# The end of a macaron encoder layer: the last product's sums, row scalings and stores in an order of their own

## The chip, the cores and the metric

The kernel runs on one core of one Trainium2 chip. The metric is the device time of one execution in microseconds (us). The profile is one execution, recorded by the hardware profiler; its span is the time from the first to the last instruction. TensorE does the matmuls, VectorE (DVE), ScalarE (ACT) and GpSimd (POOL) the elementwise work, and SyncE (SP) issues transfers.

## The reference, cut to what matters

Two sequences of 512 tokens with 1024 channels go through one encoder layer in float32, each by itself:

```python
x = x + 0.5 * swiglu(rms_norm(x, ffn1_norm), ffn1_w_gate, ffn1_w_up, ffn1_w_down)
...  # attention and mLSTM branches, merged, added to x
x = x + 0.5 * swiglu(rms_norm(x, ffn2_norm), ffn2_w_gate, ffn2_w_up, ffn2_w_down)
return rms_norm(x, final_norm)
```

where `rms_norm(x, g)` is `x * rsqrt(mean(x*x) + 1e-6) * g` over the 1024 channels, and `swiglu(x)` is `(silu(x @ w_gate) * (x @ w_up)) @ w_down` with 2816 hidden channels. The change is in the last line of this, the final norm, and in how the reciprocal root of every norm is worked out.

## The kernel before, in words

Every float32 matmul is done as three passes of rounded parts (high x high, high x low, low x high). Both sequences go through a feed-forward together, and the two-by-two product of (sequence, half) blocks is done with seven block products in place of eight, named B11, B21, T2, T3, T4, T1 and B22. The sums of these products give the four blocks of the result.

`ffn_down` (L435) is the second matmul of a feed-forward. It goes over four chunks of hidden channels, and in each over the seven products in the order of `DOWN` (L430): 28 steps. A step has four groups d = 0 to 3, one for each block of 128 tokens; a group ends in one PSUM bank, and `flush_` (L527) takes it from there: DVE adds half of it to an accumulator in SBUF (L536). In the last chunk the accumulators become the finished rows: `xs[s][:, h*4 + b]` holds sequence s, half h of the channels, block b of the tokens, 128 x 512 numbers. The finished blocks come in this order, and for each `done(s, h, b)` is called: B21 gives (0, 0), T4 gives (0, 1), T1 gives (1, 1), and B22, the very last step, gives (1, 0). So the first sequence is complete after T4, and the second block by block during B22. `e16` and `e5` are accumulators that are no longer needed in the last chunk, once their values have been added.

`done2` (L1328) ends the second feed-forward. For each block ACT squares it and sums the squares along the row into `ssq3[s]` (L1145, `square`); then POOL multiplies it by the gain `fn[h]` in place (L1331), or DVE where (s, h) is (1, 0). The multiply writes where the square reads, so it comes behind the square. When a row's two halves are there, `row_scale` (L1150) adds the two sums of squares and `rstd_cols` (L149) makes the reciprocal root r on DVE: mean plus epsilon, a first guess from the bits (a shift, a subtraction from a constant), and three rounds of three Newton instructions each, 12 small instructions, 13 with the sum. For the first sequence this is done once, for four blocks, behind its last square; for the second in two pairs of blocks, behind d = 1 and d = 3 of B22. Each block of 128 rows is then scaled by r, 128 x 1024 in one instruction, on ACT (L1345), the last block on DVE (L1343), and stored with one 512 KB transfer that SP issues (L1346). `rstd_cols` is called by all other norms of the kernel too: 21 calls in all, among them the first normalisation of each sequence (`norm_x`, L1173) and the eight memory heads, whose r TensorE broadcasts (`bcast_psum`, L181).

What sets the order: the program's instructions are put into one queue per engine by a scheduler at build time. It goes by priority, which is program order unless `shifted` changes it, and by when it believes the operands ready; an instruction that is ready goes ahead of an earlier one that isn't. On the chip each engine runs its queue strictly in order. `pin` (`tc.keep_in_program_order`, L1118) keeps the instructions that it is given in program order among each other on their engine. Nothing in `done2` is pinned before the change. The small tiles of `rstd_cols` take turns in five buffers (tag `rs4`).

Of the kernel before, what the change touches and what calls it, by code (L numbers as in the profile page):

```python
# [26 lines left out]
def encoder(ctx, tc, I, outs):  # L27
# [14 lines left out]
    def nm(s):  # L42
        n_id[0] += 1
        return f"{s}_{n_id[0]}"
# [98 lines left out]
    def emit_hl(src, g, k, xh, xl):  # L143
# [2 lines left out]
                                       op0=ALU.mult, op1=ALU.subtract)  # L146
        return i1, i2

    def rstd_cols(v, width, n):  # L149


        def t_(dt=F32):
            w = max(width, 4)
            return spool.tile([P, w], dt, tag=f"rs{w}", bufs=5, name=nm("rs"))[:, 0:width]
        V = nc.vector
        a = t_()
        V.tensor_scalar(a, v, 1.0 / n, EPS, op0=ALU.mult, op1=ALU.add)
        b = t_(I32)
        V.tensor_scalar(b, a.bitcast(I32), 1, None, op0=ALU.logical_shift_right)
        y_ = t_(I32)  # L160
        V.tensor_scalar(y_, b, -1.0, 1597463007.0, op0=ALU.mult, op1=ALU.add)
        y = y_.bitcast(F32)
        for _ in range(3):
            t = t_()
            V.scalar_tensor_tensor(t, y, -0.5, y, op0=ALU.mult, op1=ALU.mult)
            V.tensor_tensor(t, t, a, op=ALU.mult)
            r = t_()
            V.scalar_tensor_tensor(r, t, 1.5, y, op0=ALU.add, op1=ALU.mult)
            y = r
        return y  # L170

    def col_sums(acc, bs=(0, 1, 2, 3)):
        p = PT()
# [258 lines left out]
    DH = KD // 2  # L432
    n_steps = len(DOWN) * len(CHUNKS)

    def ffn_down(wd, rb, ring, tail, xres, done, at_step, hook):  # L435
# [91 lines left out]
        def flush_(i, d, p):  # L527
# [2 lines left out]
                   T3: xs[1][:, DH + d], B22: xs[1][:, d]}[m]  # L530
            if last and m == T1:
                acc = xs[1][:, DH + d]
            if i < 7 and m in (B11, T2_, T1):
                nc.scalar.activation(acc, p, AF.Copy, scale=0.5)
            else:
                V_.scalar_tensor_tensor(acc, p, 0.5, acc, op0=ALU.mult, op1=ALU.add)  # L536
# [705 lines left out]
    nhl = [None, None]  # L1242
    ssq1, ssq2, ssq3 = [[sums_tile() for _ in range(2)] for _ in range(3)]

    def done1(s, h, b):
        x_ = xs[s][:, h * 4 + b, :]
        nc.sync.dma_start(xbuf[s][:, h, b, :], x_)
        square(x_, ssq1[s][:, h, b:b + 1])
# [76 lines left out]
        for half in range(2):  # L1325
            nc.gpsimd.dma_start(fn[half], I["final_norm"][half * S:(half + 1) * S].partition_broadcast(P))

    def done2(s, h, b):  # L1328
        x_ = xs[s][:, h * 4 + b, :]
        square(x_, ssq3[s][:, h, b:b + 1])  # L1330
        (V_ if (s, h) == (1, 0) else G_).tensor_tensor(x_, x_, fn[h], op=ALU.mult)  # L1331
        if s == 0 and h == 1 and b == 3:
            n = slice(0, 4)
        elif s == 1 and h == 0 and b % 2:
            n = slice(b - 1, b + 1)
        else:
            return
        r = row_scale(ssq3[s], n)
        for i in range(n.start, n.stop):
            v = xs[s].rearrange("p (h b) c -> p h b c", h=2)[:, :, i, :]  # L1340
            r_ = r[:, i - n.start:i - n.start + 1]
            if s and i == 3:
                V_.tensor_scalar(v, v, r_, None, op0=ALU.mult)  # L1343
            else:
                nc.scalar.activation(v, v, AF.Copy, scale=r_)  # L1345
            nc.sync.dma_start(outs[s][0, i * P:(i + 1) * P, :].rearrange("p (h c) -> p h c", h=2), v)  # L1346

    ffn_down(I["ffn2_w_down"][0], rbuf[1], up.ring, tail, lambda s, h: x2buf[s][:, h], done2, n_steps - 14, load_fn)


def host_consts():
# [62 lines left out]
```

## Time and profile before

| | us |
|---|---|
| median of 3 runs (2123.21 to 2124.66) | 2124.43 |
| the profiled execution | 2124.45 |
| its span | 2122.7 |
| mean granted TensorE clock in it | 0.994 of full |

A row of the timeline reads: start in us from the span's start, duration, engine, line of the kernel, operation, what it writes and reads, shapes, how many instructions are merged in the row (x4), and in brackets how long the engine sat idle before it and what it waited for. A row of the engine table gives busy time, share of the span and number of instructions. PE is TensorE, PEld its weight loads, SPq SyncE's queue. A row of the waits reads: who waited, for what, us in total, times, longest. A row of a source view gives shortest, median and longest duration in ns; its last line, for a line that issues transfers, the time from issue to landing. In the DMA view, GB/s is the mean in the window asked for, here one in which stores were waiting throughout.

### The profile page before, as it was taken

What the parts mean: (1) busy time and instruction counts of PE and PEld (TensorE: products, weight loads), DVE (VectorE), ACT (ScalarE), POOL (GpSimd) and SP (SyncE); (2) the same over time, 40 slices, a digit from 0 to 9 for tenths busy, and PEclk for the clock granted to TensorE, in tenths of its full rate; (3) what the DMA queues carried; (4) which work ended last, traced back from release to release, by engine and by line L of the source; (5) the groups of instructions that cost most, each with busy time, mean ns of one, the idle gap of its engine ahead of it and who ended that gap; (6) DMA issues with size and microseconds to landing.
All of it is one profiled execution on the core that took longest, in us unless ns stands there. A gap on an engine that the chain in (4) does not pass through costs nothing.

```text
span 2122.7 us, 26809 instructions
## 1 busy us (share of the span) xinstructions
PE 2070.4 (98%) x9472; PEld 1687.7 (80%) x9472; DVE 1581.2 (74%) x2817; ACT 968.5 (46%) x1739; POOL 107.2 (5%) x110
## 2 busy tenths in 40 slices
PE   6999999999999999999999999999999999999997
PEld 5887788888888777878887787788777888888885
DVE  7888787776796796574668855764988887786696
ACT  6544444442225466464435654544644444443223
POOL 0000000001000110100102001010000000000002
PEclk9999999999999999999999999999999999999998
DMA  8455554389764212232342122354454554479753
GB/s 272 150 195 194 182 188 144 133 300 395 270 230 158 74 66 68 92 114 88 120 158 80 60 90 74 135 171 157 164 194 163 199 172 159 144 262 389 287 205 121
DMA packets 141270, 361.81 MB, mean 170 GB/s; under 512 B 15600, under 2 KB 15616, under 8 KB 140112
## 3 DMA queue, kind: packets, MB, share of 16 engines
q1 hardware_dynamic: 140544, 358.84, 48.0%
q0 software_dynamic: 592, 1.27, 0.3%
q8 instruction: 74, 1.21, 0.2%
q14 instruction: 60, 0.49, 0.1%
HBM read 255.15 MB, written 104.89 MB: 170 GB/s over the span
## 4 chain that ended last, share of the span: by engine, by line
PE 81%; DVE 10%; ACT 4%; DMA 4%; issue 2%; POOL 0%; SPq 0%; ACTq 0%; DVEq 0%; POOLq 0%
PE pss L278 15%; PE mm L672 14%; PE pst L278 9%; PE mm L519 8%; PE mm L278 7%; PE pst L519 4%; PE pss L519 4%; PE mm L656 4%; PE mm L1099 3%; PE pso L519 3%; DMA rbuf<-t 2%; PE pso L926 2%; PE pso L656 1%; PE pso L1055 1%; PE pst L919 1%
## 5 line engine op out<-in xcount | busy, mean ns | idle before, releaser
L672 PE MATMUL mm<-xh,w 128*128 128x512 f32 x896 | 292.6, 396 | 0.0
L278 PE MATMUL pss<-xc,w 128*128 128x512 f32 x1056 | 258.1, 391 | 6.7 <-DVE t L307 6.5
L278 PE MATMUL mm<-xc,w 128*128 128x512 f32 x1056 | 256.2, 391 | 3.0 <-ACT f L287 2.6
L278 PE MATMUL pst<-xc,w 128*128 128x512 f32 x1056 | 255.4, 390 | 0.0
L278 PEld LDWEIGHTS pss<-xc,w 128*128 128x128 f32 x1056 | 196.5, 188 | 54.2 <-DVE t L307 13.6
L278 PEld LDWEIGHTS mm<-xc,w 128*128 128x128 f32 x1056 | 196.7, 188 | 47.7 <-ACT f L287 6.9
L278 PEld LDWEIGHTS pst<-xc,w 128*128 128x128 f32 x1056 | 197.3, 188 | 43.2 <-ACT t L311 2.5
L203 DVE TENSOR_TENSOR w<-wr,w 128x1024 fp32r<-128x1024 f32 (+1 forms) x112 | 135.9, 1215 | 105.5 <-ACT w L202 104.8
L672 PEld LDWEIGHTS mm<-xh,w 128*128 128x128 f32 x896 | 168.0, 189 | 32.2
L519 PE MATMUL mm<-w,rt 128*128 128x512 f32 x792 | 185.3, 389 | 0.0
L672 PE MATMUL mm<-xl,w 128*128 128x512 f32 x448 | 177.0, 395 | 0.0
L519 PEld LDWEIGHTS mm<-w,rt 128*128 128x128 f32 x792 | 148.4, 188 | 30.8
L240 ACT ACTIVATE w<-t 128x512 fp32r<-128x512 f32 x176 | 107.0, 628 | 121.3 <-DVE t L262 42.1
L202 ACT ACTIVATE w<-wr 128x1024 fp32r<-128x1024 f32 (+1 forms) x112 | 114.4, 1028 | 98.7 <-PE mm L672 29.3
L241 DVE TENSOR_TENSOR w<-t,w 128x512 fp32r<-128x512 f32 x176 | 118.1, 689 | 45.5 <-ACT w L240 42.4
L278 PE MATMUL pss<-xc,f 128*128 128x512 f32 x528 | 128.5, 392 | 0.0
L278 PEld LDWEIGHTS pss<-xc,f 128*128 128x128 f32 x528 | 98.2, 188 | 23.6 <-DVE t L315 3.6
L576 ACT ACTIVATE w<-wr 128x512 fp32r<-128x512 f32 x72 | 44.7, 631 | 132.2 <-PE pso L519 64.2
L576 ACT ACTIVATE w<-t 128x512 fp32r<-128x512 f32 x82 | 51.6, 632 | 116.0 <-PE pst L519 47.3
L672 PEld LDWEIGHTS mm<-xl,w 128*128 128x128 f32 x448 | 84.5, 189 | 15.7
L519 PE MATMUL pss<-w,rt 128*128 128x512 f32 x396 | 94.0, 389 | 0.0
L519 PE MATMUL pst<-w,rt 128*128 128x512 f32 x396 | 93.7, 389 | 0.0
(316 smaller groups left out, 3645.9 us busy)
## 6 DMA issues: line engine op xcount, KB each, us to landing
rt<-rbuf SPq DMA_DIRECT2D x154, 512.0 KB, 5.4
wr<-in_ffn_w_gate_dram SPq DMA_DIRECT2D x56, 512.0 KB, 4.3
wr<-in_w_in_cols_dram SPq DMA_DIRECT2D x56, 512.0 KB, 3.5
rbuf<-tab SPq DMA_DIRECT2D x90, 256.0 KB, 3.3
wr<-in_ffn_w_up_dram SPq DMA_DIRECT2D x44, 512.0 KB, 4.1
rbuf<-t SPq DMA_DIRECT2D x88, 256.0 KB, 3.3
rbuf<-f SPq DMA_DIRECT2D x66, 256.0 KB, 3.2
rbuf<-R SPq DMA_DIRECT2D x64, 256.0 KB, 3.1
```

Of the source, the lines that this page charges most:

```text
L202: pin(nc.scalar.activation(hi, raw, AF.Copy))
L203: pin(lo_eng.tensor_tensor(lo, raw, f(hi), op=ALU.subtract))
L240: pin(nc.scalar.activation(t[:, 0], src, AF.Copy))
L241: pin(V_.tensor_tensor(t[:, 1], src, f(t[:, 0]), op=ALU.subtract))
L278: nc.tensor.matmul(p, a[:, k, :], xt[:, b, k, :], start=(first and k == 0 and i == 0), stop=(k == HK_ - 1 and i == 2), skip_group_check=True)
L519: nc.tensor.matmul(p, r[:, b, d * P:(d + 1) * P], u[:, a, :], start=(first and q == 0 and k == 0), stop=(q == len(us) - 1 and k == 2), ski ...
L576: nc.scalar.activation(hi, src, AF.Copy)
L656: nc.tensor.matmul(p[b][:, :N], a[:, k, bs], w_[:, kl, :], start=(k == 0 and i == 0), stop=(k == KD - 1 and i == 2))
L672: nc.tensor.matmul(p, a[:, k, :], b, start=(k == 0 and i == 0), stop=(k == n - 1 and i == 2))
L919: nc.tensor.transpose(p[:, b * P:(b + 1) * P], Ps[b][:, kb * P:(kb + 1) * P], ident)
L926: nc.tensor.matmul(po, Vst[:, kv_, hk, :], w, start=(kv_ == 0 and i == 0), stop=(kv_ == 3 and i == 1))
L1099: nc.tensor.matmul(p[b], a[:, k, bs], w_[:, k - k0, :], start=(k == 0 and i == 0), stop=(k == KD - 1 and i == 2))
```

## The change

Three things change. First, `rstd_cols` makes one Newton round of three instructions and then one round of a higher order with five, in place of three Newton rounds: 11 instructions, not 12; the part behind mean and epsilon is a function of its own, `rstd_of`, which can pin its instructions. This holds for every norm in the kernel. Second, `done2` and the new `ends2`, called for B22 in place of flush and `done`, lay out the end. Third, the last two stores of ACT's results are issued by ACT.

- The first sequence: squares and POOL multiplies as before, r for all four blocks behind T4. Its four scalings, all on ACT, are no longer issued at once, but one behind each square of T1, pinned there; each is followed by its 512 KB store on SP.
- T1's blocks, half 1 of the second sequence: ACT squares (pinned), and DVE, not POOL, multiplies by the gain into `e5` (`spare`, later `pre1`).
- B22, d = 0 to 2, all pinned: DVE's flush; ACT's square; DVE multiplies by the gain into `e16` (`pre0`). Behind d = 1: `half_ms`, which is the other half's sums times 1/1024 plus epsilon, and `last_scale(0)`, r for blocks 0 and 1 in 11 instructions. Behind d = 2's square: ACT scales the two halves of block 0, each 128 x 512, with a 256 KB store on SP.
- B22, d = 3, pinned: the flush in two halves of 256 columns; the first half is squared by ACT, the second by DVE, whose sum is added into `half_ms`; ACT scales block 1's halves; `last_scale(2)` gives r for blocks 2 and 3; then DVE scales the one half of block 3 with gain and r in one instruction while ACT scales the other and issues its store itself; DVE scales one half of block 2, ACT the other, again with a store of its own.

```diff
+    def rstd_of(a, width, pin=lambda i: i):
+        ...
+        b = t_(I32)
+        pin(V.tensor_scalar(b, a.bitcast(I32), 1, None, op0=ALU.logical_shift_right))
+        y_ = t_(I32)
+        pin(V.tensor_scalar(y_, b, -1.0, 1597463007.0, op0=ALU.mult, op1=ALU.add))
+        y = y_.bitcast(F32)
+        t = t_()
+        pin(V.scalar_tensor_tensor(t, y, -0.5, y, op0=ALU.mult, op1=ALU.mult))
+        pin(V.tensor_tensor(t, t, a, op=ALU.mult))
+        pin(V.scalar_tensor_tensor(t, t, 1.5, y, op0=ALU.add, op1=ALU.mult))
+        y, t, p, q = t, y, b.bitcast(F32), t_()
+        pin(V.tensor_tensor(t, y, y, op=ALU.mult))
+        pin(V.tensor_tensor(t, t, a, op=ALU.mult))
+        pin(V.tensor_scalar(p, t, 0.375, -1.25, op0=ALU.mult, op1=ALU.add))
+        pin(V.tensor_tensor(p, p, t, op=ALU.mult))
+        pin(V.scalar_tensor_tensor(q, p, 1.875, y, op0=ALU.add, op1=ALU.mult))
+        return q
+
     def rstd_cols(v, width, n):
-        ...
-        for _ in range(3):
-            t = t_()
-            V.scalar_tensor_tensor(t, y, -0.5, y, op0=ALU.mult, op1=ALU.mult)
-            V.tensor_tensor(t, t, a, op=ALU.mult)
-            r = t_()
-            V.scalar_tensor_tensor(r, t, 1.5, y, op0=ALU.add, op1=ALU.mult)
-            y = r
-        return y
+        a = rs_tile(width)
+        nc.vector.tensor_scalar(a, v, 1.0 / n, EPS, op0=ALU.mult, op1=ALU.add)
+        return rstd_of(a, width)
...
@@ flush_, in ffn_down
+            if last and m == B22 and ends:
+                ends(d, p, acc, e16, e5)
+                return
...
             elif m == T1:
-                done(1, 1, d)
+                done(1, 1, d, e5)
...
+    def store(s, i, h, v, q=None):
+        return (q or nc.sync).dma_start(outs[s][0, i * P:(i + 1) * P, h * S:(h + 1) * S], v)
+
-    def done2(s, h, b):
+    def done2(s, h, b, spare=None):
         x_ = xs[s][:, h * 4 + b, :]
+        if s == 0:
+            square(x_, ssq3[s][:, h, b:b + 1])
+            G_.tensor_tensor(x_, x_, fn[h], op=ALU.mult)
+            if h and b == 3:
+                other_r.append(row_scale(ssq3[0]))
             return
-        ...
+        pin(nc.scalar.activation(T2(F32, "f2"), x_, AF.Square, accum_out=ssq3[1][:, 1, b:b + 1]))
+        V_.tensor_tensor(spare[:, b], x_, fn[1], op=ALU.mult)
+        v = xs[0].rearrange("p (h b) c -> p h b c", h=2)[:, :, b, :]
+        pin(nc.scalar.activation(v, v, AF.Copy, scale=other_r[0][:, b:b + 1]))
+        nc.sync.dma_start(outs[0][0, b * P:(b + 1) * P, :].rearrange("p (h c) -> p h c", h=2), v)
+
+    def last_scale(b0):
+        a = rs_tile(2)
+        sq, hm = ssq3[1][:, 0, b0:b0 + 2], half_ms[0][:, b0:b0 + 2]
+        pin(V_.scalar_tensor_tensor(a, sq, 1.0 / D, hm, op0=ALU.mult, op1=ALU.add))
+        return rstd_of(a, 2, pin)
+
+    def ends2(b, p, acc, pre0, pre1):
+        H = S // 2
+        ssq = ssq3[1][:, 0, b:b + 1]
+        junk = T2(F32, "f2")
+
+        def on_act(i, h, r, q=None):
+            v = (pre0, pre1)[h][:, i]
+            pin(nc.scalar.activation(v, v, AF.Copy, scale=r))
+            pin(store(1, i, h, v, q))
+
+        if b < 3:
+            pin(V_.scalar_tensor_tensor(acc, p, 0.5, acc, op0=ALU.mult, op1=ALU.add))
+            pin(nc.scalar.activation(junk, acc, AF.Square, accum_out=ssq))
+            pin(V_.tensor_tensor(pre0[:, b], acc, fn[0], op=ALU.mult))
+            if b == 1:
+                t = half_ms[0] = spool.tile([P, 4], F32, tag="cs4", bufs=4, name=nm("hm"))
+                pin(V_.tensor_scalar(t, ssq3[1][:, 1], 1.0 / D, EPS, op0=ALU.mult, op1=ALU.add))
+                first_r.append(last_scale(0))
+            if b == 2:
+                for h in range(2):
+                    on_act(0, h, first_r[0][:, 0:1])
+            return
+        for c in (slice(0, H), slice(H, S)):
+            pin(V_.scalar_tensor_tensor(acc[:, c], p[:, c], 0.5, acc[:, c], op0=ALU.mult, op1=ALU.add))
+            if c.start == 0:
+                pin(nc.scalar.activation(junk[:, c], acc[:, c], AF.Square, accum_out=ssq))
+        hm = half_ms[0][:, 3:4]
+        more = spool.tile([P, 4], F32, tag="cs4", bufs=4, name=nm("more"))[:, 0:1]
+        pin(V_.scalar_tensor_tensor(junk[:, H:], acc[:, H:], 1.0, acc[:, H:], op0=ALU.mult, op1=ALU.mult, accum_out=more))
+        pin(V_.scalar_tensor_tensor(hm, more, 1.0 / D, hm, op0=ALU.mult, op1=ALU.add))
+        for h in range(2):
+            on_act(1, h, first_r[0][:, 1:2])
+        r = last_scale(2)
+        pin(V_.scalar_tensor_tensor(acc, acc, r[:, 1:2], fn[0], op0=ALU.mult, op1=ALU.mult))
+        on_act(3, 1, r[:, 1:2], nc.scalar)
+        pin(store(1, 3, 0, acc))
+        pin(V_.tensor_scalar(pre1[:, 2], pre1[:, 2], r[:, 0:1], None, op0=ALU.mult))
+        pin(store(1, 2, 1, pre1[:, 2]))
+        on_act(2, 0, r[:, 0:1], nc.scalar)
```

More of the change, by code (lines that the diff above doesn't have):

```diff
@@ L433, in encoder, with ffn_down @@
     n_steps = len(DOWN) * len(CHUNKS)
-    def ffn_down(wd, rb, ring, tail, xres, done, at_step, hook):
+    def ffn_down(wd, rb, ring, tail, xres, done, at_step, hook, ends=None):
         n = n_steps
@@ L1351, in host_consts @@
+    ffn_down(I["ffn2_w_down"][0], rbuf[1], up.ring, tail, lambda s, h: x2buf[s][:, h], done2, n_steps - 14, load_fn,
+             ends2)
 def host_consts():
```

37 lines of the change are left out of this document (8 added, 29 removed).

## The prediction, made before the changed kernel had run

> **What bounds the kernel now.** I read the page's engine table first, then the end of the timeline, then the source and DMA views of the stores, and last TensorE's waits over the whole run.
>
> ```profile
> PE 2070.4 (98%) x9472; PEld 1687.7 (80%) x9472; DVE 1581.2 (74%) x2817; ACT 968.5 (46%) x1739; POOL 107.2 (5%) x110
> ```
>
> TensorE is busy 2070.4 of 2122.7 us, so an edit wins only where TensorE waits or behind its last matmul. TensorE's own timeline of the end:
>
> ```profile
> 2091.57 6.28 PE L519 MATMUL mm<-w,rt 128*128 128x512 f32 x27
> 2097.69 2.20 PE L519 MATMUL pso<-w,rt 128*128 128x512 f32 x9
> 2099.73 6.28 PE L519 MATMUL mm<-w,rt 128*128 128x512 f32 x27
> 2105.85 2.20 PE L519 MATMUL pso<-w,rt 128*128 128x512 f32 x9
> ```
>
> A product (four groups d = 0 to 3, nine matmuls each) takes 2099.73 - 2091.57 = 8.16 us, a group 2.04. T1 starts at 2091.57, the last product, B22, at 2099.73; its last group ends at 2105.85 + 2.20 = 2108.05. The other engines from there:
>
> ```profile
> 2101.97 0.69 DVE L536 SCALAR_TENSOR_TENSOR xs<-mm,xs 128x512 f32<-128x512 f32 x1 [1.35 <-PE mm L519]
> ...
> 2110.90 0.68 DVE L536 SCALAR_TENSOR_TENSOR xs<-pso,xs 128x512 f32<-128x512 f32 x1
> ...
> 2113.05 0.15 DVE L1154 TENSOR_TENSOR rsum<-sqs 128x2 f32<-128x2 f32 x1
> ...
> 2115.48 0.16 DVE L168 SCALAR_TENSOR_TENSOR rs<-rs,rs 128x2 f32<-128x2 f32 x1
> 2115.74 1.15 ACT L1345 ACTIVATE xs<-xs,rs 128x1024 f32<-128x1024 f32 x1 [1.02 <-DVE rs L168]
> ```
>
> ```profile
> 2116.91 1.20 SPq L1346 DMA_DIRECT2D out_dram<-xs  x2
> ```
>
> The flush of d = 3 (L536) starts at 2110.90, 2.85 us after its matmuls: DVE runs in order and has the first r chain of the second sequence in front. The second chain goes from its row sums (2113.05) to its last step (2115.48), 13 instructions 0.20 us apart. The last scaling on ACT ends at 2116.89, and the last two stores leave from 2116.91 on, their issues together 1.20 us.
>
> ```profile
> L1346 SPq DMA_DIRECT2D out_dram<-xs x8: 533/534/650, 2099.6 to 2117.5; - x8
> ...
> DMA to landing us min/median/max: 3.1/3.3/4.2
> ```
>
> ```profile
> DMA packets 206, 0.39 MB, mean 389 GB/s; under 512 B 16, under 2 KB 16, under 8 KB 206
> ```
>
> ```profile
> L1410 SPq DRAIN  x3: 7/7/7, 2121.8 to 2122.1; - x3
> ```
>
> Issuing a 512 KB store takes 0.53 to 0.65 us, and it lands 3.1 us after its issue at best. The last store, queued behind its neighbour, is the 4.2 of this row: 2116.91 + 0.65 + 4.2 = 2121.8, where SP's drains begin; 0.9 us later, at 2122.7, the span ends. The engines move 389 GB/s while stores wait, so 256 KB cost 0.67 us. The 14.65 us behind the last matmul are thus DVE's order (2.85), chain and scaling (6.0), and stores and drain (5.8).
>
> **The change, part by part.** Times are on the clock of this trace, as if TensorE ended its products when it does now.
>
> *T1, 2091.6 to 2099.7.* DVE's and POOL's rows, and ACT's:
>
> ```profile
> 2093.36 1.29 POOL L1331 TENSOR_TENSOR xs<-xs,tab 128x512 f32<-128x512 f32 x1 [0.50 <-ACT f L1145]
> 2093.51 1.16 DVE L157 TENSOR_SCALAR rs<-rsum 128x4 f32<-128x4 f32 x1
> ...
> 2094.99 0.69 DVE L536 SCALAR_TENSOR_TENSOR xs<-mm,xs 128x512 f32<-128x512 f32 x1
> ```
>
> ```profile
> 2098.39 4.27 ACT L1345 ACTIVATE xs<-xs,rs 128x1024 f32<-128x1024 f32 x4 [1.89 <-DVE rs L168]
> 2102.56 0.61 ACT L1145 ACTIVATE f<-xs 128x512 f32<-128x512 f32 x1
> 2103.08 0.18 ACT L1145 ACTIVATION_READ_ACCUMULATOR f<-xs 128x1 f32 x1
> 2103.18 0.62 ACT L1145 ACTIVATE f<-xs 128x512 f32<-128x512 f32 x1
> ...
> 2104.40 0.62 ACT L1145 ACTIVATE f<-xs 128x512 f32<-128x512 f32 x1
> ```
>
> Four columns wide, L157 lasts 1.16 us and ends with the POOL multiply beside it (2093.36 + 1.29 = 2094.65): POOL held DVE. After the change POOL's multiplies of the second sequence are DVE's, four of 0.69 into e5. This hold stays, since its POOL operation belongs to the first sequence; any later one goes. Of the first sequence's chain, which now ends at 2098.3 (the scalings wait for it until 2098.39), eight steps are left behind the flush at 2094.99: 2094.99 + 0.6 + 8 x 0.20 = 2097.2, and 0.6 more if one of the new multiplies slips in between, as this flush did. I take one: **r at 2097.8**.
>
> Today four scalings 1.04 apart take ACT in one block, and the square of the last product's d = 0, whose flush ends at 2101.97 + 0.69, waits until 2104.40. In the new order scalings and squares (0.61 apart) alternate: 4 x 1.04 + 3 x 0.61 = 6.0 us from r, ACT free at 2103.8. DVE has 3 flushes and at most 4 multiplies left behind r, 4.3 us, and is done when the last product's first sum comes. The four stores of the first sequence leave 1.65 us apart against 1.35 of data each and are over before the next: no cost.
>
> *B22, d = 0 and 1.* d = 1 is done on TensorE at 2101.97 + 2.04 = 2104.01. Flush 0.69, link to ACT 0.10 (2115.48 + 0.16 to 2115.74): square at 2104.80. Its accumulator is out 0.70 later (2102.56 to 2103.08 + 0.18); 0.06 for the link to DVE starts the chain at 2105.56. ACT is free in time. The first half's row sums are prepared ahead (half_ms), so the chain has 11 steps: r for blocks 0 and 1 at 2105.56 + 10 x 0.20 + 0.16 = 2107.72. The multiply by the gain goes to another tile, needs no square, and hides under it; without that cover it would cost 0.69.
>
> *B22, d = 2 and 3.* The pins fix the order: **the flush of d = 2, ready on TensorE at 2106.05, stands behind the whole chain**, a new wait to 2107.63. Behind it stand all later steps of DVE and, through its square, all of ACT. A 256-wide DVE operation costs half of this:
>
> ```profile
> 730.74 0.76 DVE L577 TENSOR_TENSOR t<-t,t 128x256 fp32r<-128x256 f32 x2
> ```
>
> ACT: square of d = 2 at 2107.63 + 0.79 = 2108.42, block 0's two scalings at 2109.03 and 2109.56 (0.53 apart, half of 1.04), the half square of d = 3 at 2110.09, its accumulator out at about 2110.55. DVE: flush 2107.63, gain 2108.24, two half flushes from 2108.85, the other half's square from 2109.5 (0.38 each), its sum in half_ms by 2110.2. ACT is last; the second chain runs from 2110.6 to 2112.75, and block 1's scalings (2110.4 to 2111.6) hide under it. Were they late, its last step would wait for them, since it may write the buffer they read.
>
> *The end.* ACT's scaling of block 3 starts 0.26 after the last step's start, as in L168 to L1345 above, 2112.85 to 2113.5 (as long as a square, 0.62); DVE's fused scaling beside it ends at 2113.5 too. Both halves of block 3 are issued then. ACT scales a half of block 2 behind its own issue, DVE the other. The trace has no DMA issued by ACT; the bounds are SP's issue of this size and POOL's:
>
> ```profile
> L1247 SPq DMA_DIRECT2D xbuf<-xs x16: 319/320/320, 624.4 to 671.9; - x16
> ...
> DMA to landing us min/median/max: 2.0/2.0/4.6
> ```
>
> ```profile
> 1.24 1.10 POOL L123 DMA_DIRECT2D g<-in_ffn_norm_dram  x1 [0.81 <-POOLq L1401]
> ```
>
> With 0.32 the last store's issue starts at 2113.5 + 0.32 + 0.63 + 0.1 = 2114.55, with 1.10 at 2115.3. I take 0.32, the row of the same size; 1.10 would cost up to 0.6, since that issue itself is 0.78 longer (2115.3 + 0.78 + 2.4 = 2118.5 against the 2117.9 below). The four stores then queue for the engines: the first lands 2.0 us (this row) to 2.4 us (3.1 - 0.67) after 2113.5, the other three need 3 x 0.67 = 2.0 more. With 2.4 the last lands at 2117.9, and 0.95 more ends the span at **2118.9 against 2122.7: 3.8 us less**; with 2.0 it is 4.2.
>
> The Trainium skill, DMA: Bandwidth & Descriptors, Rules for kernel authors, speaks against the two issues on ScalarE: spreading DMAs over issuing engines wins no bandwidth, as all share the same 16 engines, only the sequencer's issue time. By that rule they are worth nothing here, and the sum stays as it is, since it books nothing for them: an issue (0.32) is shorter than a store's data (0.67). No run so far shows it.
>
> *The shorter chain everywhere, 12 steps to 11.* What of it TensorE waits for:
>
> ```profile
> PE pss L1140 <- DVE raw L1188: 13.6, 2, 11.2
> ...
> PE pst L185 <- DVE rs L168: 1.6, 4, 0.5
> ...
> PE pst L185 <- DVE rs L157: 0.6, 2, 0.3
> ```
>
> The first normalisation is exposed at the start (a wait of 11.2 us ends with it): 0.2. The broadcasts in the memory heads waited six times, 2.2 us: up to 6 x 0.2 = 1.2 goes. I book half, since DVE's queue holds other work between the steps. The other chains release no wait of TensorE, they lie beside its matmuls: nothing, and 0.2 each where that cover is gone. Together **0.8**, between 0 and 1.4; below 0 only if the shift changes DVE's order (rival 1).
>
> **Sum.** 3.8 + 0.8 = 4.6. The profiled execution took 2124.45 us, 1.75 outside its span, and the median is 2124.43, so one working serves both: 2124.45 - 4.6 = 2119.85, rounded **2119.9**.
>
> **Rivals.**
>
> 1. *The tail alone*: the shift of 0.2 us reorders DVE's queue somewhere ahead and gives back what the shorter chain wins. For it: most of TensorE's waits have other releasers. Against it: six rows wait for this very chain. 2124.45 - 3.8 = 2120.7.
>
> 2. *The first sequence's r comes late* (the other side). Its chain isn't pinned, and ACT's scalings and squares now wait behind it in order. ACT has 0.3 us in hand, so from r = 2098.1 on every us is lost at the end. If all flushes and multiplies of T1 go ahead, the last waits for TensorE until 2099.93: 2099.93 + 2 x 0.69 + 1.6 = 2102.9, 4.8 late, 2119.85 + 4.8 = 2124.7: slower than before. With three slipped in, r is at 2099.0 and the time 2120.8. Against it: today one slips in.
>
> 3. *More is won*: landing in 2.0 and all of the 1.4: 2124.45 - 4.2 - 1.4 = 2118.85.
>
> 4. *The second queue is dear*: stores issued by another engine land late. The far bound is POOL's:
>
> ```profile
> tab<-in_final_norm_dram POOLq DMA_DIRECT2D x2, 256.0 KB, 7.7
> ```
>
> The last store from ACT would land at 2114.55 + 7.7 = 2122.25, the span end 0.5 later than now, and the time be 2124.45 + 0.5 - 0.8 = 2124.15. SP's 2.0 for the same size is the nearer row; a third of the way gives 2121.3.
>
> **How the numbers follow.** About 0.2% (4.2 us) is what a measurement of this kernel can tell from no change; the line lies at 2120.2, near my forecast. Forecast (2119.2 to 2120.6) 0.52, of it 0.36 below the line; tail alone 0.18, within; r late 0.10, of it 0.03 slower by over 0.2% (with a reordering ahead on top); more won 0.13, faster; second queue 0.07, within but for 0.01. Faster 0.49, same 0.47, slower 0.04. Range: from 2118.2 (more won, and 0.65 of small links) to 2122.4 (tail alone, r at 2099.0, ACT's issue slow, and 0.2 of small links: 2120.7 + 0.9 + 0.6 + 0.2).
>
> **What would show it.** r of the first sequence before 2098.2, scalings and squares alternating on ACT, no POOL operation after 2095; the flush of d = 2 right behind the last step of the first two-wide chain, 1.6 us after its matmuls; the second chain starting 2.5 us after the last matmul, as the half square's accumulator is read; four stores back to back; 10.5 to 11.2 us behind the last matmul instead of 14.65; and the last matmul up to 1.4 us earlier. Wrong would be another length behind the last matmul, or an end of TensorE that comes later.

## The result, and the profile after

The changed kernel took 2119.45 us (median of 10 runs, 2117.53 to 2121.86), the one before 2123.96 (10 runs on the same chip, 2121.95 to 2128.45): a ratio of 0.9975, 95% interval 0.9966 to 0.9984, or 5.3 us less, give or take 1.9. (The medians alone differ by 4.5; the ratio is near that of the means.) The profiled execution took 2120.39 us, its span is 2118.6.

| us | before | after | change | forecast |
|---|---|---|---|---|
| end of the last matmul | 2108.05 | 2107.19 | -0.86 | -0.8 |
| from there to the end of the span | 14.65 | 11.41 | -3.24 | -3.8 |

The profile after, TensorE's last row in the timeline of the end:

```profile
2104.99 2.20 PE L526 MATMUL pso<-w,rt 128*128 128x512 f32 x9
```

The last matmul ends at 2104.99 + 2.20 = 2107.19. All experiments below are measured from this point. To compare two traces, shift one until these ends agree: a time of after gets 0.86 on before's clock.

The same view, DVE and ACT from the first sequence's chain on:

```profile
2094.84 0.69 DVE L1352 TENSOR_TENSOR e<-xs,tab 128x512 f32<-128x512 f32 x1
...
2096.31 0.68 DVE L546 SCALAR_TENSOR_TENSOR xs<-mm,xs 128x512 f32<-128x512 f32 x1
...
2097.02 0.69 DVE L1352 TENSOR_TENSOR e<-xs,tab 128x512 f32<-128x512 f32 x1
2097.63 0.16 DVE L171 SCALAR_TENSOR_TENSOR rs<-rs,rs 128x4 f32<-128x4 f32 x1
...
2097.88 1.16 ACT L1354 ACTIVATE xs<-xs,rs 128x1024 f32<-128x1024 f32 x1 [2.26 <-DVE rs L171]
...
2103.90 0.61 ACT L1379 ACTIVATE f<-xs 128x512 f32<-128x512 f32 x1
...
2107.23 0.16 DVE L171 SCALAR_TENSOR_TENSOR rs<-rs,rs 128x2 f32<-128x2 f32 x1
2107.31 0.68 DVE L1378 SCALAR_TENSOR_TENSOR xs<-mm,xs 128x512 f32<-128x512 f32 x1
...
2108.08 0.63 ACT L1379 ACTIVATE f<-xs 128x512 f32<-128x512 f32 x1 [2.86 <-DVE xs L1378]
...
2108.71 1.32 ACT L1374 ACTIVATE e<-e,rs 128x512 f32<-128x512 f32 x2
...
2109.94 0.40 ACT L1392 ACTIVATE f<-xs 128x256 f32<-128x256 f32 x1
...
2110.46 0.16 DVE L1361 SCALAR_TENSOR_TENSOR rs<-sqs,hm 128x2 f32<-128x2 f32 x1 [0.42 <-ACT f L1392]
...
2112.51 0.16 DVE L171 SCALAR_TENSOR_TENSOR rs<-rs,rs 128x2 f32<-128x2 f32 x1
2112.70 0.72 ACT L1374 ACTIVATE e<-e,rs 128x512 f32<-128x512 f32 x1 [1.05 <-DVE rs L171]
...
2113.45 0.40 ACTq L1341 DMA_DIRECT2D out_dram<-e  x1
...
2113.90 0.72 ACT L1374 ACTIVATE e<-e,rs 128x512 f32<-128x512 f32 x1 [0.47 <-ACT e L1374]
...
2114.65 0.34 ACTq L1341 DMA_DIRECT2D out_dram<-e  x1
```

The first sequence's r is ready at 2097.63 + 0.16 = **2097.79**, which is 2098.65 on before's clock. Wide DVE operations stand among the chain's last steps, two multiplies (L1352) and a flush (L546). ACT waits 2.26 us for that r with its four scalings still to come, and works through to the last product's squares (2103.90). The flush of d = 2 (2107.31) comes right behind the last step of the first two-wide chain (2107.23), 2.16 us after its matmuls, which end one group (2.04) before the last. The second chain starts at 2110.46, 3.27 us after the last matmul (5.00 before: 2113.05 - 2108.05), and ends at 2112.67; the last store is issued from 2114.65 on, and the span ends 3.95 later. From the last matmul on, the 3.24 us are then:

| us | before | after | change |
|---|---|---|---|
| to the start of the second chain | 5.00 | 3.27 | -1.73 |
| the chain (13 steps, 11 steps) | 2.59 | 2.21 | -0.38 |
| scaling, to the start of the last store's issue | 1.92 | 1.98 | +0.06 |
| that issue, landing and drain | 5.14 | 3.95 | -1.19 |

The DMA view of after's last 22 us gives issues by form: count, KB of one, median us from issue to landing.

```profile
out_dram<-e SPq DMA_DIRECT2D x5, 256.0 KB, 2.1
out_dram<-e ACTq DMA_DIRECT2D x2, 256.0 KB, 2.9
```

ACT's two stores queue behind others and still land 2.9 us after their issue; before, the queued 512 KB took 4.2. And TensorE's waits for a chain of r, over the whole run of after (total us, times, longest):

```profile
PE pss L1150 <- DVE raw L1198: 12.8, 2, 10.6
...
PE pst L192 <- DVE rs L171: 1.1, 3, 0.5
...
PE pst L192 <- DVE rs L176: 0.4, 2, 0.2
```

The memory heads' broadcasts (L192) wait 1.5 us in five times, against 2.2 in six before. The waits at the start (L1150) are 0.8 shorter, 12.8 against 13.6.

### The profile page after: what moved, and what is told of

It is laid out like the page before. It is cut to its first block, busy times and chain, and to the rows that moved or that the text cites. A ratio compares the mean times of both kernels' runs of the same rounds, so it can differ in the third digit from the quotient of the medians.

```text
span 2118.6 us, 26805 instructions
## 1 busy us (share of the span) xinstructions
PE 2072.1 (98%) x9472; PEld 1689.7 (80%) x9472; DVE 1578.7 (75%) x2803; ACT 968.4 (46%) x1742; POOL 95.9 (5%) x106
## 4 chain that ended last, share of the span: by engine, by line
PE 83%; DVE 9%; DMA 4%; ACT 3%; issue 2%; POOL 0%; SPq 0%; ACTq 0%; DVEq 0%; POOLq 0%
PE pss L285 15%; PE mm L682 14%; PE pst L285 10%; PE mm L526 8%; PE mm L285 8%; PE pst L526 4%; PE pss L526 4%; PE mm L666 4%; PE mm L1109 3%; PE pso L526 3%; PE pso L936 1%; PE pso L666 1%; DMA rbuf<-t 1%; PE pso L1065 1%; PE pss L910 1%
```

## The experiments

Two theories stood against each other at first. **Order**: the gain is what the new order does behind the last matmul, plus a little for the shorter chain. **Chain**: the shorter chain does more of it, spread over the run. Within the first the question was what sets the second chain's start: the late r, the flush of d = 2, or the stores. Unless another is named, an edit is made to the changed kernel. The length behind the last matmul ("the end" below) was 11.36 to 11.42 us in the five kernels of this document whose code of the end is that of the change or differs only in who issues two stores, while executions of one kernel differ in time by 2 us and more. So each verdict names which of the two it rests on. Each end is read from one profiled execution, and its span is given to 0.1 us. The kernels with stores on SP, with one block, with multiplies on POOL and with nine more steps ran once; of them only the end is used.

**The two halves by themselves.** The kernel before with the chain of 11 steps alone:

```diff
-        for _ in range(3):
-            ...
-        return y
+        return rstd_of(a, width)
```

> The kernel before with the shorter chain alone. My theory (the order of the end wins most, the shorter chain the rest): the end of the last matmul comes 0.6 to 0.9 us earlier than in the profile before (2108.05), and behind it two exposed chains are one step shorter, 14.65 - 0.4 = 14.25 us; the time is 1.0 to 1.3 us below before. Rival A (the shorter chain does most of it): 3 us or more below. Rival B (the 0.86 us in front is only how executions differ): last matmul where it was, time 0.4 us below.

The end took 14.13 us, and the time was 0.9987 of before (0.9979 to 0.9996). The other half, the new order with three Newton rounds in every chain:

```diff
-        pin(V.tensor_tensor(t, y, y, op=ALU.mult))
-        ...
-        pin(V.scalar_tensor_tensor(q, p, 1.875, y, op0=ALU.add, op1=ALU.mult))
+        for o in (p, q):
+            pin(V.scalar_tensor_tensor(t, y, -0.5, y, op0=ALU.mult, op1=ALU.mult))
+            pin(V.tensor_tensor(t, t, a, op=ALU.mult))
+            pin(V.scalar_tensor_tensor(o, t, 1.5, y, op0=ALU.add, op1=ALU.mult))
+            y = o
```

> The changed kernel with three Newton rounds again in every chain, 12 steps. My theory: behind the last matmul 11.43 us + 2 x 0.20 + up to 0.2 for the first sequence's r = 11.8 to 12.05, the last matmul back near 2108.05, the time 2.6 to 2.9 us below before. Rival A: 1 us or less below before. Rival B: last matmul near 2107.2 as in the changed kernel.

The end took 12.06 us, the time was 0.9990 (0.9981 to 0.9999). Both ends came as expected. Of the 3.24 us at the end, the order with the old chain makes 14.65 - 12.06 = 2.59, and the shorter chain 0.52 (alone) to 0.65 (on top of the order): the two add up. In the whole time the shorter chain is worth more than that: alone 2.8 us (0.9 to 4.5), where the theory had 1.0 to 1.3 and rival A 3 or more. The interval holds both, and the order alone won 2.1 (0.2 to 4.0), so the whole time doesn't rank the two halves; the end does. The last matmul ended at 2107.77 with the chain alone and at 2108.54 with the order alone, against 2107.19 after and 2108.05 before.

**Who issues the last stores.** SP instead of ACT:

```diff
-        on_act(3, 1, r[:, 1:2], nc.scalar)
+        on_act(3, 1, r[:, 1:2])
...
-        on_act(2, 0, r[:, 0:1], nc.scalar)
+        on_act(2, 0, r[:, 0:1])
```

> The changed kernel with its last two stores issued by SP, not ACT. My theory, and the rule of the Trainium skill (DMA: Bandwidth & Descriptors, Rules for kernel authors) that another issuing engine wins no bandwidth: behind the last matmul 11.4 us within 0.2, since the four stores queue for the engines either way; ACT's last scaling starts 0.5 us earlier, as no issue is in front of it. Rival: the second queue shortens the end, and without it 0.4 us or more come back.

11.40 us against 11.41: the second issuing queue wins and costs nothing. ACT's row of this kernel's timeline, and the last two issues:

```profile
2111.25 1.33 ACT L1374 ACTIVATE e<-e,rs 128x512 f32<-128x512 f32 x2 [1.05 <-DVE rs L171]
...
2112.89 0.89 SPq L1341 DMA_DIRECT2D out_dram<-e  x2
```

Without issues of its own ACT does both scalings in a row, 1.33 us in all. In after the second begins 1.20 after the first (2112.70, 2113.90), 0.6 later than here. But here its store stands last in SP's queue: SP starts its last issue at 2113.4, 7.70 us behind the last matmul (2105.70), and in after ACT starts it at 7.46. That store lands 2.7 us after its issue and in after 2.9 (the longest of each kernel's source view), so what is left of the difference is gone at the end. This fits the expectation that the four stores queue for the engines either way. It is also what the Trainium skill says in DMA: Bandwidth & Descriptors, Rules for kernel authors, that spreading DMAs over issuing engines saves sequencer time only; the trace agrees, 11.40 against 11.41.

**Scalings between the squares, or in one block.** All four scalings of the first sequence at once, behind r, as before the change:

```diff
                 other_r.append(row_scale(ssq3[0]))
+                for i in range(4):
+                    v = xs[0].rearrange("p (h b) c -> p h b c", h=2)[:, :, i, :]
+                    pin(nc.scalar.activation(v, v, AF.Copy, scale=other_r[0][:, i:i + 1]))
+                    nc.sync.dma_start(outs[0][0, i * P:(i + 1) * P, :].rearrange("p (h c) -> p h c", h=2), v)
...
-        v = xs[0].rearrange("p (h b) c -> p h b c", h=2)[:, :, b, :]
-        pin(nc.scalar.activation(v, v, AF.Copy, scale=other_r[0][:, b:b + 1]))
-        nc.sync.dma_start(outs[0][0, b * P:(b + 1) * P, :].rearrange("p (h c) -> p h c", h=2), v)
```

> The changed kernel with the first sequence's four scalings in one block on ACT, as before, and not one behind each square of T1. My theory: ACT has the same work in front of the last product's squares (four scalings of 1.04 and the squares), so it is free at the same time and the stretch behind the last matmul stays 11.4 us within 0.2. Rival (the interleaving is what frees ACT): 1 us or more longer.

The end took 10.91 us: half a microsecond less than with the change's order, which neither the theory nor the rival had. ACT's timeline in this kernel:

```profile
2096.30 0.64 ACT L1355 ACTIVATE f<-xs 128x512 f32<-128x512 f32 x1 [2.48 <-DVE rs L163]
...
2098.49 0.63 ACT L1355 ACTIVATE f<-xs 128x512 f32<-128x512 f32 x1 [1.47 <-DVE rs L170]
...
2099.29 4.28 ACT L1352 ACTIVATE xs<-xs,rs 128x1024 f32<-128x1024 f32 x4
...
2104.70 0.62 ACT L1380 ACTIVATE f<-xs 128x512 f32<-128x512 f32 x1
```

Two squares of T1 are done ahead of the scalings here, while r is still being made; in after one. There the square of d = 1, whose flush ended at 2096.31 + 0.68 = 2096.99, stands behind the first scaling, which waits for r until 2097.88. ACT reaches the last product's first square at 2104.70 here. Its last matmul:

```profile
2106.39 2.20 PE L526 MATMUL pso<-w,rt 128*128 128x512 f32 x9
```

That ends at 2108.59, 1.40 later than in after, so on after's clock the square starts at 2103.30 against 2103.90. The change's interleaving **holds up one square**, which moves ACT by 0.6 us and the end by 0.5: an instruction that waits at the head of an in-order queue holds up the ready one behind it.

**When the first sequence's r is ready.** Three edits move it. T1's multiplies back on POOL:

```diff
-        V_.tensor_tensor(spare[:, b], x_, fn[1], op=ALU.mult)
+        G_.tensor_tensor(spare[:, b], x_, fn[1], op=ALU.mult)
```

> The changed kernel with T1's four multiplies by the gain on POOL again, into e5. My theory: two multiplies of 0.6 us no longer slip into the first sequence's chain, but POOL holds its small steps once or twice, about 1.0 each; r comes within 0.8 us of where it is (2097.8), and the stretch behind the last matmul is 11.4 us within 0.7. Rival (moving them off POOL is what wins): 1 us or more longer.

The first sequence's chain unbroken: its sum, mean and steps pinned in a row, and T1's flushes issued behind its last step. (A pin queues an instruction behind the one written just before it on its engine; what isn't pinned can still slip between, as T1's flushes and multiplies do in after.)

```diff
+            elif last and m == T1 and ends:
+                with tc.issue_after(chain_end[0].ins):
+                    V_.scalar_tensor_tensor(acc, p, 0.5, acc, op0=ALU.mult, op1=ALU.add)
...
-                other_r.append(row_scale(ssq3[0]))
+                s_ = spool.tile([P, 4], F32, tag="cs4", bufs=4, name=nm("rsum"))
+                pin(V_.tensor_tensor(s_, ssq3[0][:, 0], ssq3[0][:, 1], op=ALU.add))
+                a = rs_tile(4)
+                pin(V_.tensor_scalar(a, s_, 1.0 / D, EPS, op0=ALU.mult, op1=ALU.add))
+                other_r.append(rstd_of(a, 4, keep))
```

> The changed kernel with the first sequence's chain unbroken in DVE's queue and T1's flushes behind it. My theory: r at about 2095.9 in place of 2097.8; the square of the last product's d = 1 then waits for its flush and not for ACT, 0.55 us earlier, and the stretch behind the last matmul is 11.43 - 0.55 = 10.9 us; the time 0.5 us below the changed kernel. Rival: ACT is not what sets the second half's chain, 11.4 stays.

And three more Newton rounds, nine steps, in this one chain:

```diff
+        for i in range(more):
+            V.scalar_tensor_tensor(t, y, -0.5, y, op0=ALU.mult, op1=ALU.mult)
+            V.tensor_tensor(t, t, a, op=ALU.mult)
+            V.scalar_tensor_tensor(o[i % 2], t, 1.5, y, op0=ALU.add, op1=ALU.mult)
+            y = o[i % 2]
...
-                other_r.append(row_scale(ssq3[0]))
+                other_r.append(row_scale(ssq3[0], more=3))
```

> The changed kernel with three more Newton rounds, nine steps, in the first sequence's chain alone (they change nothing but the time). My theory (rival 2 of the prediction as a price): r is 1.8 us later by the steps and 0.6 to 1.2 more by wide operations that slip in, and every us is lost at the end, since ACT's scalings and squares wait in order: behind the last matmul 13.8 to 14.5 us, about all that the change won there. Rival (the first sequence's scalings have slack): 11.4 to 12.

| r ready, on after's clock | kernel | the end, us |
|---|---|---|
| 2095.79 | chain unbroken | 10.95 |
| 2097.38 | multiplies on POOL | 11.03 |
| 2097.79 | the change | 11.41 |
| 2100.57 | nine more steps | 14.23 |

In the kernel with nine more steps, the timeline's rows of DVE's last step, of ACT's first scaling behind it and of the last matmul:

```profile
2098.59 0.16 DVE L185 SCALAR_TENSOR_TENSOR rs<-rs,rs 128x4 f32<-128x4 f32 x1
...
2098.85 1.16 ACT L1364 ACTIVATE xs<-xs,rs 128x1024 f32<-128x1024 f32 x1 [5.05 <-DVE rs L185]
...
2103.17 2.20 PE L536 MATMUL pso<-w,rt 128*128 128x512 f32 x9
```

r is ready at 2098.59 + 0.16 = 2098.75, and the last matmul ends at 2105.37, 1.82 earlier than in after, so 2100.57 on its clock. It is 2.78 later than in after, and the end is 2.82 longer: **one for one**. On the other side the gain stops: r 2.0 earlier brings 0.46. If it is one for one up to there, a late r begins to cost at 2097.79 - 0.46 = 2097.33 on after's clock; the forecast had 2098.1 on before's, which is 2097.24. All three ends came as expected (up to 0.7 from 11.4, 10.9, 13.8 to 14.5); the time of the unbroken chain was 0.9971 (0.9959 to 0.9984).

The kernel with POOL's multiplies also shows what DVE and POOL hold from each other. Its timeline:

```profile
2091.86 1.29 POOL L1352 TENSOR_TENSOR e<-xs,tab 128x512 f32<-128x512 f32 x1 [1.10 <-DVE rs L163]
...
2091.89 1.28 DVE L164 TENSOR_TENSOR rs<-rs,rs 128x4 f32<-128x4 f32 x1
...
2095.04 3.79 POOL L1352 TENSOR_TENSOR e<-xs,tab 128x512 f32<-128x512 f32 x3 [1.89 <-DVE xs L546]
...
2096.05 0.69 DVE L546 SCALAR_TENSOR_TENSOR xs<-pso,xs 128x512 f32<-128x512 f32 x1 [0.49 <-PE pso L526]
```

A chain step of 0.16 us (L164, two SBUF operands) takes 1.28 beside a POOL multiply that began just before it, and ends with it. A flush (L546, one operand in PSUM) takes its usual 0.69 in the midst of three POOL multiplies. The Trainium skill, SBUF — State Buffer, SBUF: two separate sides, has the rule: a DVE operation with two SBUF inputs and a GpSimd operation take a shared pair of ports as a lock for the whole instruction. The trace agrees, with 1.28 beside 1.29, and 0.69 where only one input lies in SBUF. Even so this kernel's r is 0.41 earlier than in after: from the first Newton step (L163) to the last (L171) the one hold cost 1.1 here, and two multiplies and a flush in between cost 1.5 there (2.91 us, from 2094.72 to 2097.63, for what takes seven steps of 0.20).

**The flush of d = 2.** It goes ahead of the first two-wide chain, the half square of d = 3 ahead of block 0's scalings, and block 2's multiply by the gain into the fused scaling at the end:

```diff
-            pin(V_.tensor_tensor(pre0[:, b], acc, fn[0], op=ALU.mult))
+            if b < 2:
+                pin(V_.tensor_tensor(pre0[:, b], acc, fn[0], op=ALU.mult))
...
-                first_r.append(last_scale(0))
             if b == 2:
-                for h in range(2):
-                    on_act(0, h, first_r[0][:, 0:1])
+                first_r.append(last_scale(0))
...
-        for h in range(2):
-            on_act(1, h, first_r[0][:, 1:2])
+        for i in range(2):
+            for h in range(2):
+                on_act(i, h, first_r[0][:, i:i + 1])
...
-        pin(V_.tensor_scalar(pre1[:, 2], pre1[:, 2], r[:, 0:1], None, op0=ALU.mult))
-        pin(store(1, 2, 1, pre1[:, 2]))
-        on_act(2, 0, r[:, 0:1], nc.scalar)
+        a2 = xs[1][:, 2]
+        pin(V_.scalar_tensor_tensor(a2, a2, r[:, 0:1], fn[0], op0=ALU.mult, op1=ALU.mult))
+        on_act(2, 1, r[:, 0:1], nc.scalar)
+        pin(store(1, 2, 0, a2))
```

> The changed kernel with the flush of d = 2 ahead of the first two-wide chain, the half square of d = 3 ahead of block 0's scalings on ACT, and no gain multiply of block 2 ahead of the second chain (DVE scales that half with gain and r in one instruction at the end). My theory: the second chain starts at 2109.25 on the changed kernel's clock in place of 2110.46, and the stretch behind the last matmul is 11.43 - 1.2 = 10.2 us. Rival (the end is set by the stores and the drain, not by the chain's start): within 0.4 of 11.4.

The end took 10.26 us, as expected, and the time was 0.9974 of before (0.9964 to 0.9983). In this kernel's timeline:

```profile
2103.74 2.20 PE L526 MATMUL pso<-w,rt 128*128 128x512 f32 x9
...
2108.11 0.16 DVE L1361 SCALAR_TENSOR_TENSOR rs<-sqs,hm 128x2 f32<-128x2 f32 x1
```

The second chain starts 2108.11 - 2105.94 = 2.17 us behind the last matmul against 3.27 in after, 1.10 earlier, and the end is 1.15 shorter. The pins thus have a price, but this run changes three things at once and doesn't part the flush from ACT's square and the multiply. Then the unbroken first chain together with the last two of these edits, and the two-wide chain ahead of the flush as in the change:

```diff
+            if b == 2:
+                first_r.append(last_scale(0))
             pin(V_.scalar_tensor_tensor(acc, p, 0.5, acc, op0=ALU.mult, op1=ALU.add))
```

> The changed kernel with the first sequence's chain unbroken, block 2's gain multiply dropped and ACT's half square ahead of block 0's scalings, but the first two-wide chain ahead of the flush of d = 2 as in the change. My theory: that chain starts at 2104.7, the flush of d = 2 at 2106.8, the flush of d = 3 at 2107.4 (its matmuls end at 2107.2), the second chain at 2108.7, 1.75 us earlier than in the changed kernel: 9.7 us behind the last matmul, time 5.5 to 6 us below before. Rival: the seven stores in flight hold the last ones, 10.3 or more.

The same rows of this kernel, and its last store:

```profile
2105.73 2.20 PE L526 MATMUL pso<-w,rt 128*128 128x512 f32 x9
...
2109.66 0.16 DVE L1373 SCALAR_TENSOR_TENSOR rs<-sqs,hm 128x2 f32<-128x2 f32 x1
...
2113.78 0.34 ACTq L1344 DMA_DIRECT2D out_dram<-e  x1
```

The end took 10.07 us, the shortest of all, but 0.4 over what was expected: the second chain starts 1.73 after the last matmul (2109.66 - 2107.93; 1.5 expected), and the span ends 4.22 behind the last issue (2118.0 - 2113.78), 0.27 more than in after. The end lies between the theory's 9.7 and the rival's 10.3. Against the unbroken chain alone (10.95) the last two edits give 0.88, with the flush of d = 2 still behind the chain (2107.55, behind 2107.47). All three gave 1.15 above, so little may be left for the flush's place itself; no run moves it alone. The time is 0.9971 of before (0.9958 to 0.9984), not to be told from the change's 0.9975.

**Where the rest of the shorter chain's gain comes from.** If the ends are as measured, what the whole time leaves over is the front. If each step of a chain costs in front, adding steps must show it. Two and four more rounds, 6 and 12 steps, in the 18 chains ahead of the end:

```diff
-    def rstd_cols(v, width, n):
+    def rstd_cols(v, width, n, more=2):
...
-                other_r.append(row_scale(ssq3[0]))
+                other_r.append(row_scale(ssq3[0], more=0))
```

> The changed kernel with two more Newton rounds, six more steps of 0.20 us, in the 18 chains ahead of the end; the chains of the end stay short. The rounds change nothing but the time. My theory: each of these chains lasts 1.2 us longer; the start gives 1.2 and the eight memory heads most of 8 x 1.2, one rope chain up to 1.2: the last matmul 7 to 12 us later, 1.2 to 2.0 us for each step of 0.2 us. Behind the last matmul unchanged, 11.4. Rival B (what lies in front doesn't depend on the chain): last matmul within 2 us of 2107.2.

> The changed kernel with four more Newton rounds, 12 more steps of 0.20 us, in the 18 chains ahead of the end (they change nothing but the time); the end's chains stay short. Behind the last matmul 11.4. With six more steps TensorE's waits for these chains grew by 1.5 us, not by the 8 x 1.2 that I had expected. Theory now: what a step costs depends on what the scheduler can lay beside the chain; with 2.4 us a chain that cover runs out in some heads: 2 to 6 us slower than the changed kernel, ratio to before 0.999 to 1.001. Rival (the length of these chains doesn't count in front): ratio 0.997 to 0.9985.

And the three Newton rounds of before in those chains, the 11 steps at the end alone:

```diff
-        return rstd_of(a, width)
+        return (rstd_of if short else rstd_three)(a, width)
```

> The changed kernel with 12 steps, three Newton rounds, in the 18 chains ahead of the end, as before the change, and the short chains at the end. Behind the last matmul 11.4, so what is left of the ratio is the front alone. Theory (the booked 0.8 us, as the waits on the chain in the profiles have it, 2.2 us before and 1.5 after): ratio 0.9976 to 0.9983, 0.3 to 1.5 us above the changed kernel. Rival (the front is worth 2 us, as the times of the kernels with the short chain hint): ratio 0.9984 or more.

The three ends took 11.37, 11.36 and 11.42 us: that length doesn't depend on the front. The ratios were 0.9980 (0.9971 to 0.9989), 1.0031 (1.0019 to 1.0043) and 0.9984 (0.9975 to 0.9992). The second is slower than was expected (0.999 to 1.001), and the third lies where theory and rival meet and decides nothing. Taking from each ratio (times 2125) what the end changed:

| steps of a front chain | kernels | front, us against before |
|---|---|---|
| 11 | the change; chain alone; unbroken; flush first; three edits | -2.1, -2.2, -2.5, -1.1, -1.6 |
| 12 | order alone; twelve in front | +0.5, -0.2 |
| 17 | two more rounds | -1.0 |
| 23 | four more rounds | +9.9 |

Each carries 2 to 3 us of uncertainty. The five kernels with 11 steps average -1.9 (give or take 0.9, were they independent), those with 12 steps +0.1. But 17 steps are not slower than 12, where the expectation was 7 to 12 us slower, and 23 lose 10 at a stroke: **the times show no steady price per step**. TensorE's waits do. In the kernel with 12 steps more (23), the waits at the start and the broadcasts' (L202 there) are:

```profile
PE pss L1160 <- DVE raw L1208: 17.7, 2, 13.2
...
PE pst L202 <- DVE rs L185: 3.0, 4, 0.8
...
PE pst L202 <- DVE rs L158: 1.0, 2, 0.5
```

The broadcasts wait 4.0 us, 2.5 more than in after, and the start 4.9 more. The kernel with three Newton rounds in front has, for the same two, 13.0 and 2.2:

```profile
PE pss L1172 <- DVE raw L1220: 13.0, 2, 10.6
...
PE pst L214 <- DVE rs L192: 1.6, 4, 0.5
...
PE pst L214 <- DVE rs L198: 0.6, 2, 0.3
```

The same two waits, in us, in all kernels:

| steps of a front chain | kernels | start | broadcasts |
|---|---|---|---|
| 11 | nine | 12.5 to 13.0 | 1.4 to 1.8 |
| 12 | before, order alone, twelve in front | 13.0 to 13.6 | 2.2 to 2.3 |
| 17 | two more rounds | 15.1 | 3.0 |
| 23 | four more rounds | 17.7 | 4.0 |

From 11 to 23 steps that is some 0.4 us a step at the start, where two sequences have a chain of 0.20 a step each, and 0.2 in the eight heads together. From 12 steps to 11 the waits of after and of the kernel with three rounds give 0.2 at the start and 0.7 in the heads, 0.9 in all, of the 2 us by the times. With 17 steps they are 2.3 above those of before, and the time of the front is 1.0 below it: something that these waits don't hold, scatter included, makes some 3 us between these two. (The profiled execution with 17 steps, whose last matmul ended at 2110.53, 3.3 after after's, was the slowest of ten.)

With 23 steps the last matmul ended at 2118.34, 11.15 us after after's, and the waits above make 7.4 of it. The windows view gives, for a stretch, busy time and count of PE, PEld, DVE, ACT and POOL, then the granted clock; the first 70 us of after and of the kernel with 12 more steps:

```profile
0.00:70.00 70.00, 54.02 (x245) 44.47 (x246) 55.62 (x119) 47.49 (x75) 5.10 (x12) 0.98 0.76 256
```

```profile
0.00:70.00 70.00, 49.62 (x228) 40.94 (x229) 56.31 (x138) 43.65 (x70) 5.31 (x12) 0.85 0.76 252
```

TensorE was busy 4.4 us less, about what the longer wait at the start takes. The granted clock is 0.85 instead of 0.98, but that doesn't follow the chain: with the same 11 steps in front it was 0.93 in the kernel with one block, which had done 255 matmuls by then, and 0.90 in the one with the flush first. The stretch from 680 to 800 us, ahead of the first memory head, is short of 26 matmuls:

```profile
680.00:800.00 120.00, 115.49 (x580) 91.95 (x578) 103.34 (x222) 70.39 (x144) 14.70 (x20) 1.00 0.25 80
```

```profile
680.00:800.00 120.00, 111.73 (x554) 89.43 (x552) 99.94 (x231) 63.91 (x130) 15.70 (x20) 0.97 0.26 81
```

18 of the 26 are missing between 720 and 740 us (69 against 87 matmuls, at a granted clock of 0.83 against 1.00). There TensorE transposes the rotated queries, which DVE makes behind one of the longer chains, 32 columns wide. The transposes of after and of the kernel with 23 steps:

```profile
720.31 1.06 PE L852 MATMUL pst<-ident,t 128*128 128x128 f32 x8 [1.46 <-DVE t L587]
```

```profile
729.06 1.94 PE L862 MATMUL pst<-ident,t 128*128 128x128 f32 x8 [3.38 <-DVE t L597]
```

TensorE stood idle for 3.38 us, not 1.46, and behind it the same eight matmuls took 1.94 us, not 1.06: the granted clock was 0.50 from 728 to 734 us and 0.79 in the next two. The half clock costs some 3 us (an estimate: half of the six). With the 7.4 of waits that is most of the 11.15.

The scheduler lays out the queues anew for each length of chain, so these kernels differ in more than the steps. Whether that also makes the 1 us which the times show from 12 steps to 11 and the waits don't, or whether it is scatter, stays open.

## Why the prediction was right or wrong

The mechanism was right in the main and the size near: 4.6 us forecast, 5.3 measured (3.4 to 7.2). That the sum came so near is in part luck. The end fell 0.56 short of its forecast and was, at 11.41 us, outside the 10.5 to 11.2 that the prediction had named as its sign; the front by the times gave 2.1 (give or take 1.9) and not 0.8; the two errors have opposite signs.

- *r at 2097.8, one wide operation slipped in.* Wrong by 0.85: it came at 2098.65 on before's clock, two multiplies and a flush among the last steps. This was rival 2 in a mild form, not the forecast. Its price was forecast rightly: "from r = 2098.1 on every us is lost" is the one-for-one of the four r times above. 0.55 was lost, ACT's 512-column scalings 0.60 apart and not 0.53 (with them the half square of d = 3 came 1.23 behind the first, not 1.06) added 0.17, and the second chain started 3.27 behind the last matmul, not 2.55. The way around was not seen: with the scalings in one block the wait for r would have held one square less.
- *The flush of d = 2 behind the whole chain.* Right in the order (2107.23 and 2107.31); its wait was 2.16 us and not 1.6, as the chain came late. Undone together with ACT's order and a multiply, it gave 1.15 us; the latter two without it gave 0.88 where r was early.
- *Second chain, scaling, issue.* 11 steps in 2.21 us, 2.15 forecast; from there to the last issue 1.98 and not 1.80, as ACT's issue took 0.40 and not 0.32 and its scaling 0.72 and not 0.63.
- *ACT's issue at 0.32, stores landing 2.0 to 2.4.* The issue takes 0.34 to 0.40. The landing was the better end of the bound: 3.95 us from the last issue to the end of the span against 4.35. Rival 4, the dear second queue, fell with the run that moved the stores to SP (11.40).
- *The sum of the end.* +0.72 for the late chain start, +0.24 for chain to issue, -0.40 for landing: 11.41 in place of 10.85.
- *The front, 0.8.* The waits that it named bear it out: 0.7 in the heads (2.2 to 1.5; 0.6 booked), and 0.2 at the start against the kernel with three rounds in front (0.8 against before). By the times of five kernels it was 1.9, give or take 0.9, so the term may be short by some 1 us that no wait shows. The profile's 0.86 is no proof of either: with the same front code the last matmul ended at 2104.17 in one kernel (multiplies on POOL) and at 2108.75 in another (chain unbroken). Rival 1, that a reordering ahead eats this gain, did not come about at 11 steps.

## What to carry to other kernels

Price an end from the last matmul on, engine by engine in queue order: that length can be read to 0.1 us where the time scatters by 2, and each experiment here could be judged by it. An instruction that waits at the head of an in-order queue charges its wait to every ready one behind it, so work that needs a late result goes behind all that does not: here one square ahead of the scalings was worth 0.5 us. A shorter chain that all parts of a kernel call changes the whole queue layout, and most callers hide it: by TensorE's waits a step was worth 0.6 us here, not 18 x 0.2. So its worth is read from the waits that end with it, and the time has to be measured by itself.

## What the runs showed of the hardware

The granted clock of the first 70 us differed between kernels whose front has the same code: 0.98 in after, 0.93 with one block, 0.90 with the flush first; it was 0.93 before and 0.85 with 12 more steps. Later in that last kernel an idle time of 3.38 us on TensorE was followed by about six us at half the granted clock, and one of 1.46 in after by none. The last four stores were over at the same time with two of them issued by ACT and with all issued by SP (11.41 and 11.40 us behind the last matmul); ACT did nothing else for 0.47 us around its issue of 0.40. How much a DVE step loses beside POOL goes by its operands: 1.1 us with both in SBUF (1.28 for L164), 1.0 with its only one there (1.16 for L157 before), nothing with one in PSUM (0.69 for a flush).
